# A transformer block in split fp32: planned operation list, transposed copy of x, parameters as columns

## The chip, the cores and the metric

One core of one Trainium2 chip runs the whole block. The metric is device time in microseconds (us), the median of the runs; lower is better. The core has five engines with a queue of their own each: TensorE (PE, matrix products), VectorE (DVE), ScalarE (ACT), GpSimd (POOL) and SyncE (SP), which here only issues DMA transfers. Each works its queue in order.

## The reference

The input x is 256 rows of 2048 channels. Three residual steps follow one another.

```python
f = swiglu(rmsnorm(h, ln_ffn1_pre), ffn1_gate, ffn1_up, ffn1_down)   # 2048 -> 5632 -> 2048
h = h + 0.5 * rmsnorm(f, ln_ffn1_post)
p = rmsnorm(h, ln_mix_pre) @ w_in           # RWKV-7 input, pooling input, two gates
y_a = rwkv7(p[...]) @ w_proj_a              # a scan over 256 steps, 16 heads of 64
y_b = pool(p[...]) @ w_proj_b               # moving averages over 2, 4, 8, 16 rows
m = sigmoid(g_a) * y_a + sigmoid(g_b) * y_b
h = h + rmsnorm(m @ w_out, ln_mix_post)
f = swiglu(rmsnorm(h, ln_ffn2_pre), ffn2_gate, ffn2_up, ffn2_down)
h = h + 0.5 * rmsnorm(f, ln_ffn2_post)
```

All is float32. rmsnorm(x, g) divides each row by the root of its mean square and multiplies channel by channel with g.

## The kernel before

**A product in three parts.** PE multiplies in a rounded format (F32R). Every operand is split: ACT copies it into F32R ("high", `wH`, `xH`), DVE subtracts that from the original ("low", `wL`, `xL`), and `mm3` (L178 to L180) sums high x high, high x low and low x high in one PSUM bank. So a weight tile of 128 x 1024 costs one DMA of 512 KB on SP's queue (L140), one ACT copy (L154) and one DVE subtraction (L155), for 12 matmuls of 128 x 512 on PE.

**Transposed activations.** PE wants the rows of an activation by channels. `transpose_split` (L635 to L648) turns a piece of 128 x 512 with four PE transposes, and ACT (L641) and DVE (L643) read the result out of PSUM, scaled by the gain, as high and low. Inside the feed-forward stages the hidden activations are turned on DVE instead (L653) and moved by 16 small POOL DMAs a block (L665).

**The head.** Gate block 0 of the first feed-forward is written out in `head`: 12 warm-up transposes (L514), then loads of x in pieces of 256 KB, of the gain row g1 (L1561), which one more PE transpose makes a column, and of the weights, and then for each pair of channel tiles the transposes of x between the matmuls. After its last matmul the row statistics follow (eight ACT sums of squares, L725).

**Seven products for eight.** From feed-forward block 2 on (there are 11 blocks of 512 hidden columns), `seven` computes the gate and up columns of a block together and replaces some groups of eight 128 x 512 products by seven on sums and differences of the operands (Strassen's scheme; DVE makes the differences of the weights, L407 to L415, and ACT and DVE split them, L422 and L423). At the end of such a block DVE adds the banks together (L449), the product with Silu (L750) follows, and then the turn. The banks of the gate half (`f0`, `f1`) are those that the next block starts on.

**The order of work.** In the feed-forward stages the order on PE, ACT and DVE is written out by a small planner: PE's work is a list with durations (`put`), all other operations are events with a time on PE's clock (`at`), and `run` merges the two. The times are constants written by hand (for instance, the additions at a block's end at 0.7 us after the last group of seven, `AHEAD`, `CARRY`, `TURNS`). A weight tile's load, copy and subtraction are one event, at the time when a buffer comes free (`slot`: five split buffers `WS_BUFS`, four raw ones `W32_BUFS`). `run` is called once in each stage's first product. The rest (the mixer's ACT and DVE work, the products after it) is ordered by the compiler's scheduler.

**The offloaded pair.** In blocks 3 to 6 of each feed-forward (`PROBE`), one of the ten plain weight pairs does not use DVE for its low part (`low_by`, L326 to L348): its raw tile, high and low parts lie in buffers of their own; ACT copies the high part (L335). In the first feed-forward ACT also writes the negated tile (L337) and a POOL DMA accumulates onto it (L341); in the second POOL subtracts (L343).

**Parameters.** Gains and RWKV vectors come by a dozen small DMAs as rows, and two PE transposes (L936) make columns of them (`load_rows`).

Of the kernel before, what the change touches and what calls it, by code (L numbers as in the profile page):

```python
# [11 lines left out]
F32 = mybir.dt.float32  # L12
# [6 lines left out]
P = 128  # L19
# [19 lines left out]
TT = 0.45  # L39
NUNITS = 33  # L40
STAG = 10
TRAIL = 16
AHEAD = (5.0, 6.0)
TURNS = [[4.2, 5.3, 6.4, 7.5], [5.3, 6.0, 6.7, 7.4]]
WARM = 12
TB = 4
DOWN = ((0, 7, ((8, 12), (0, 3, 5, 7, 9)), 0),
        (2, 8, ((2, 4, 6, 8, 10, 12), (0, 2)), TRAIL))
OUT = ((0, 0, (), 0), (1, 2, ((4,), (0,)), 0), (3, 0, (), TRAIL))
FAST = range(2, 11)  # L50
PROBE = range(3, 7)
CARRY = (18, 21)
NG, SPOTS = 3, ((2, 4), (1,))

ROWS = [("ln_mix_pre", 16), ("ln_ffn2_pre", 16), ("mu", 26), ("w0", 8), ("a0", 8),
        ("k_k", 8), ("k_a", 8)]
ROWS2 = [("r_k", 8), ("gn_w", 8), ("gn_b", 8), ("pool_scale", 8)]


class Block:  # L60
    def __init__(s, tc, ctx):
# [5 lines left out]
        s.late, s.after, s.items, s.events, s.now = [], [], deque(), [], 0.0  # L67
        s.clk, s.uses = 0.0, []
# [35 lines left out]
    def at(s, t, fn):  # L104

        s.n += 1
        heapq.heappush(s.events, (t, s.n, fn))

    def slot(s, end):

        s.uses.append(end)
        n = len(s.uses) - 1 - WS_BUFS
        return s.uses[n] if n >= 0 else n - 1.0

    def run(s):

        s.now = 0.0
        E = mybir.EngineType
        with s.tc.manual_schedule(engines={E.PE, E.Activation, E.DVE}):
            while s.items or s.events:  # L120
                while s.events and (s.events[0][0] <= s.now or not s.items):
                    heapq.heappop(s.events)[2]()
                if s.items:
                    t, fn = s.items.popleft()
                    fn()
                    s.now += t
            s.stats()
        s.now = s.clk = 0.0
        s.uses = []

    def put(s, t, fn):
        s.items.append((t, fn))
        s.clk += t
# [48 lines left out]
    def gemm_tok(s, w, c0, at, KT, evac, lead=False, trail=False, xs=None, hold=False,  # L182
                 order=None):
        pss = [s.pm.tile([P, 512], F32, tag="mm", name=s.nm("mm")) for _ in range(2)]
        ws = {}

        def do(k, h):
            (wH, wL), (xH, xL) = ws[k], at(k)
            s.mm3(pss[h], xH[:, h * P:h * P + P], xL[:, h * P:h * P + P], wH, wL,
                  k == 0, k == KT - 1)  # L190

        def keep(tiles):
            ws.update((k, (wH, wL)) for k, wH, wL in tiles)

        def both(k0, k1):
            for k2 in order or range(k0, k1, 4):
                keep(s.load_w(w, k2, min(4, k1 - k2), c0, 512))
                for k in range(k2, min(k2 + 4, k1)):
                    do(k, 0)
                    do(k, 1)  # L200

        if trail:
            both(0, KT - TRAIL)
            s.by_half(w, c0, KT - TRAIL, KT, s.clk, AHEAD[0], do, keep,
                      lambda h: evac(h, pss[h]))
            return
        k0 = 0
        if xs:
            s.head(w, c0, KT, do, keep, xs)
            k0 = KT  # L210
        elif lead:
            s.by_half(w, c0, 0, STAG, s.clk, AHEAD[1], do, keep)
            s.run()
            k0 = STAG
        both(k0, KT)
        if hold:
            for h in range(2):
                s.at(0.3 + 1.6 * h, lambda h=h: evac(h, pss[h]))
            return
        with s.tc.high_priority(offset=BOOST):  # L220
            for h in range(2):
                evac(h, pss[h])

    def gemm_at(s, w, c0, at, KT, evac):

        pss = []
        ws = {}

        def load(k):
            ws.update((i, (wH, wL)) for i, wH, wL in s.load_w(w, k, 2, c0, 512))  # L230

        def do(k):
            if not pss:
                pss.extend(s.pm.tile([P, 512], F32, tag="mm", name=s.nm("mm"))
                           for _ in range(2))
            for h in range(2):
                (wH, wL), (xH, xL) = ws[k], at(k)
                s.mm3(pss[h], xH[:, h * P:h * P + P], xL[:, h * P:h * P + P], wH, wL,
                      k == 0, k == KT - 1)
        for k in range(0, KT, 2):  # L240
            s.at(s.slot(s.clk + 12 * MM), lambda k=k: load(k))
            s.put(6 * MM, lambda k=k: do(k))
            s.put(6 * MM, lambda k=k: do(k + 1))
        for h in range(2):
            s.at(s.clk + 0.3 + 1.6 * h, lambda h=h: evac(h, pss[h]))

    def by_half(s, w, c0, k0, k1, start, ahead, do, keep, done=None):

        for k in range(k0, k1, 2):
            s.at(start + (k - k0) * 3 * MM - ahead,  # L250
                 lambda k=k: keep(s.load_w(w, k, 2, c0, 512, k - k0 >= STAG)))
        for h in range(2):
# [1383 lines left out]
```

## Time and profile before

| what | us |
|---|---|
| median of 3 runs (2049.80 to 2051.21) | 2050.68 |
| profiled execution, span from first to last instruction | 2047.8 |
| PE busy | 2019.4 |
| DVE busy | 1741.7 |
| ACT busy | 1161.5 |
| POOL busy | 337.8 |

The profiled execution's span is 2.9 us below the median of the timed runs, which holds what lies around the first and last instruction. The views of the trace used below are: the page (busy time of each engine), the table of stretches (busy time, instruction counts, the granted TensorE clock as a share of full speed, share of DMA engines and GB/s for each stretch of time), the list of waits (who waited for whom), and the timeline (start, duration, engine, line, operation, output<-inputs, count, and in square brackets the idle time before it with what ended it). A matmul's stated duration covers its way through the array; the next one starts earlier, so PE can lose time between two matmuls that the busy share does not show. The distance between starts shows it.

### The profile page before, as it was taken

What the parts mean: (1) busy time and instruction counts of PE and PEld (TensorE: products, weight loads), DVE (VectorE), ACT (ScalarE), POOL (GpSimd) and SP (SyncE); (2) the same over time, 40 slices, a digit from 0 to 9 for tenths busy, and PEclk for the clock granted to TensorE, in tenths of its full rate; (3) what the DMA queues carried; (4) which work ended last, traced back from release to release, by engine and by line L of the source; (5) the groups of instructions that cost most, each with busy time, mean ns of one, the idle gap of its engine ahead of it and who ended that gap; (6) DMA issues with size and microseconds to landing.
All of it is one profiled execution on the core that took longest, in us unless ns stands there. A gap on an engine that the chain in (4) does not pass through costs nothing.

```text
span 2047.8 us, 28810 instructions
## 1 busy us (share of the span) xinstructions
PE 2019.4 (99%) x10011; PEld 1664.0 (81%) x10011; DVE 1741.7 (85%) x2296; ACT 1161.5 (57%) x1563; POOL 337.8 (16%) x681
## 2 busy tenths in 40 slices
PE   9999999999999999999999999999999999999997
PEld 7887778888888888878788788888877888888886
DVE  6998889999998867789689577869989999999986
ACT  7555555555555566675576444565555555555553
POOL 0122111211000023402320111001222213110000
PEclk9999999999999999999999999999999999999999
DMA  7667776666667777757556557666666666766674
GB/s 259 194 202 240 219 219 211 203 220 212 207 213 257 226 212 213 205 162 213 147 171 187 162 170 265 216 216 195 213 200 213 215 198 213 219 215 195 216 258 144
DMA packets 227418, 425.66 MB, mean 208 GB/s; under 512 B 24127, under 2 KB 27593, under 8 KB 227273
## 3 DMA queue, kind: packets, MB, share of 16 engines
q1 hardware_dynamic: 204137, 384.70, 60.4%
q0 software_dynamic: 22848, 38.61, 6.1%
q8 instruction: 79, 1.29, 0.3%
q10 hardware_dynamic: 288, 0.52, 0.1%
q14 instruction: 66, 0.54, 0.1%
HBM read 396.69 MB, written 8.39 MB: 198 GB/s over the span
## 4 chain that ended last, share of the span: by engine, by line
PE 81%; DVE 8%; issue 4%; DMA 3%; ACT 2%; POOL 0%; DVEq 0%; ACTq 0%; POOLq 0%; SPq 0%
PE mm L178 23%; PE mm L180 23%; PE mm L179 23%; PE ms L179 3%; PE ms L180 3%; PE ms L178 3%; DVE wL L155 2%; DMA w<-in_ffn_gate_dram 2%; DVE u L449 1%; DMA w<-in_ffn_up_dram 1%; ACT wH L154 1%; DVE t L407 1%; DVE wL L423 1%; ACT wH L422 1%; PE tr L635 1%
## 5 line engine op out<-in xcount | busy, mean ns | idle before, releaser
L178 PE MATMUL mm<-wH,xH 128*128 128x512 f32 x2200 | 859.4, 391 | 4.8 <-DVE u L449 3.7
L179 PE MATMUL mm<-wL,xH 128*128 128x512 f32 x2200 | 855.3, 389 | 5.0 <-DVE wL L155 5.0
L180 PE MATMUL mm<-wH,xL 128*128 128x512 f32 x2200 | 854.6, 388 | 0.7 <-DVE xL L643 0.7
L155 DVE TENSOR_TENSOR wL<-w,wH 128x1024 fp32r<-128x1024 f32 (+1 forms) x543 | 655.2, 1220 | 205.7 <-ACT wH L154 199.6
L154 ACT CAST wH<-w 128x1024 fp32r<-128x1024 f32 (+1 forms) x543 | 557.9, 1044 | 342.5 <-PE mm L180 245.1
L178 PEld LDWEIGHTS mm<-wH,xH 128*128 128x128 f32 x2200 | 413.4, 188 | 94.4 <-issue 6.8
L179 PEld LDWEIGHTS mm<-wL,xH 128*128 128x128 f32 x2200 | 413.5, 188 | 90.6 <-DVE wL L155 8.3
L180 PEld LDWEIGHTS mm<-wH,xL 128*128 128x128 f32 x2200 | 413.4, 188 | 86.2 <-DVE xL L643 1.5
L422 ACT CAST wH<-t 128x1024 fp32r<-128x1024 f32 x172 | 181.1, 1054 | 291.9 <-DVE t L415 172.0
L665 POOL DMA_DIRECT2D x<-T x352 | 173.0, 502 | 687.7 <-DVE T L653 317.2
L423 DVE TENSOR_TENSOR wL<-t,wH 128x1024 fp32r<-128x1024 f32 x172 | 209.6, 1221 | 10.9 <-ACT wH L422 6.4
L423 DVE TENSOR_TENSOR wL<-w,wH 128x1024 fp32r<-128x1024 f32 (+1 forms) x172 | 163.1, 948 | 1.1 <-ACT wH L422 1.1
L422 ACT CAST wH<-w 128x1024 fp32r<-128x1024 f32 (+1 forms) x172 | 140.6, 832 | 30.5 <-DMA w<-in_ffn_down_dram 15.3
L407 DVE TENSOR_TENSOR t<-w,w 128x1024 f32<-128x1024 f32 x86 | 104.8, 1218 | 2.5 <-DMA w<-in_ffn_down_dram 2.5
L179 PE MATMUL ms<-wL,sH 128*128 128x512 f32 x174 | 67.7, 389 | 0.0
L178 PE MATMUL ms<-wH,sH 128*128 128x512 f32 x174 | 67.7, 389 | 0.0
L180 PE MATMUL ms<-wH,sL 128*128 128x512 f32 x174 | 67.7, 389 | 0.0
L449 DVE TENSOR_TENSOR u<-ms,u 128x512 f32<-128x512 f32 x92 | 61.4, 686 | 1.4
L718 POOL DMA_DIRECT2D R<-R x96 | 47.2, 499 | 83.8 <-issue 57.6
L411 DVE TENSOR_TENSOR t<-w,t 128x512 f32<-128x512 f32 x86 | 58.9, 685 | 0.0
L415 DVE TENSOR_TENSOR t<-w,t 128x512 f32<-128x512 f32 x86 | 58.8, 684 | 0.0
L845 POOL DMA_DIRECT2D gb<-in_ln_ffn_post_dram x4 | 2.2, 558 | 284.7 <-PE mm L180 142.6
(333 smaller groups left out, 2068.2 us busy)
## 6 DMA issues: line engine op xcount, KB each, us to landing
w<-in_w_in_dram SPq DMA_DIRECT2D x128, 512.0 KB
w<-in_ffn_up_dram SPq DMA_DIRECT2D x122, 512.0 KB
w<-in_ffn_gate_dram SPq DMA_DIRECT2D x120, 512.0 KB
w<-in_ffn_down_dram SPq DMA_DIRECT2D x116, 512.0 KB
w<-in_ffn_down_dram SPq DMA_DIRECT2D x120, 256.0 KB
w<-in_ffn_gate_dram SPq DMA_DIRECT2D x112, 256.0 KB
w<-in_ffn_up_dram SPq DMA_DIRECT2D x108, 256.0 KB
w<-in_w_out_dram SPq DMA_DIRECT2D x28, 512.0 KB
```

The costliest lines, as they stand in the source:

```text
L154: s.nc.scalar.copy(vH, v)
L155: s.nc.vector.tensor_tensor(out=vL, in0=v, in1=vH.bitcast(F32), op=ALU.subtract)
L178: nc.tensor.matmul(ps, aH, bH, start=start, stop=False)
L179: nc.tensor.matmul(ps, aH, bL, start=False, stop=False)
L180: nc.tensor.matmul(ps, aL, bH, start=False, stop=stop)
L407: V.tensor_tensor(out=v["t13"], in0=v["a"], in1=v["b0"].to_broadcast([P, 2, 512]), op=ALU.subtract)
L411: V.tensor_tensor(out=v["t24"][:, 0], in0=v["a"][:, 0], in1=v["t13"][:, 1], op=ALU.add)
L415: V.tensor_tensor(out=v["t24"][:, 1], in0=v["b"][:, 0], in1=v["t24"][:, 0], op=ALU.subtract)
L422: nc.scalar.copy(H, v[n_])
L423: V.tensor_tensor(out=L, in0=v[n_], in1=H.bitcast(F32), op=ALU.subtract)
L449: V.tensor_tensor(out=u[o], in0=bank[b], in1=u[i], op=ALU.add)
L665: nc.gpsimd.dma_start(out=x[0][q * 32:q * 32 + 32, i], in_=src[i * 32:i * 32 + 32, q])
```

## The change

The order of PE's matmuls in the products is the same, and so are the numbers of the groups of seven, the buffers and the tile sizes. Different are:

- **The planner.** Every operation is a `job` with an engine, a duration from a formula, the jobs that it needs, the buffers that it takes and gives back, and a due time. `play` runs a small simulation: each of ACT, DVE, POOL and the loads takes, when free, the ready job with the earliest due time; PE takes its list in order. The order in which jobs were taken is the order in which they are issued. Two lists make up the kernel: the first feed-forward with its border into the mixer's first gate product, and the second half of `w_proj_a` with the output projection and the second feed-forward. Load, copy and subtraction of a weight tile are jobs of their own, as are the sum of squares and the mean of the row statistics, which come due 9 us after the piece that they read. The sums of the additions that free `f0` and `f1` have due times 1.0 and 1.6 us after a block's last matmul.
- **The offloaded pair is gone**: `low_by` and `PROBE` are removed, and all ten pairs of a block go through ACT and DVE.
- **The head.** A second copy of x, laid out by channels (`x_t`), is an input. `head` loads it in pieces, ACT and DVE make high and low parts of 128 x 256 straight from it, and no PE transposes stand between the matmuls. x itself (2 MB) is loaded after the gate weights, for the row statistics only.
- **Parameters** come as one laid-out array of columns (`cols`): 16 columns in a first DMA on ACT's queue, the other columns in a second; the transposes are gone.
- **Normed activations** of the first feed-forward are made from `x_t` (four DVE operations of 128 x 256) in place of high plus low and a product (two of 128 x 1024), and the sums for the groups of seven read them directly.

The core of the diff:

```diff
+LAG = dict(P=0.2, A=0.18, V=0.16, G=0.2, D=2.4, N=0.0)
+CAPS = dict(w=W32_BUFS, ws=WS_BUFS, u=1)
+FAST = {b: "fffqffqllqlll" for b in range(2, 11)}
-FAST = range(2, 11)
-PROBE = range(3, 7)
+va = lambda m: 0.07 + m / 960
+aa = lambda m: 0.09 + m / 1200
...
+    def play(s, order, wait):
+        free = dict(P=0.0, A=0.0, V=0.0, G=0.0, D=-10.0)
...
+        while True:
+            best = None
+            for e in "DAVG":
+                if now[e]:
+                    t = free[e]
+                elif soon[e]:
+                    t = max(free[e], soon[e][0][0])
+                else:
+                    continue
+                if best is None or t < best[0]:
+                    best = t, e
+            if order and not order[0].left:
+                t = max(free["P"], order[0].ready)
+                if best is None or t < best[0]:
+                    best = t, "P"
...
+            n.left = -1
+            free[e] = t + n.dur
+            n.fn()
+            done(n, t + n.dur + n.lag)
...
+    def feed(s, w, k, n, c0, t, hold=False):
...
+        g = s.job("D", 1.75 * m / 1024, get, t - 9, take=("w", b))
+        h = s.job("A", aa(m), high, t - va(m) - aa(m) - 0.5, (g,), None if hold else ("ws", b))
+        return b, s.job("V", va(m), low, t - va(m) - 0.3, (h,), give=(("w", b),))
...
         def pair(k, w, c0, b):
-            if other and (b, k) == other[1]:
-                s.low_by(other[0], w, k, c0, s.clk, keep)
-            else:
-                s.at(s.slot(s.clk + 12 * MM), lambda: keep(s.load_w(w, k, 2, c0, 512)))
+            ws, l = s.feed(w, k, 2, c0, s.clk)
...
+        t = s.clk + 1.0
+        j1, j2, j3, j4 = m
+        a0, a1 = plus(1, "f0", 1, t, j3, last["f"]), plus(3, "f1", 3, t + 0.6, j4, last["f"])
+        s.freed.update(f0=a0, f1=a1)
...
+        def part(k):
+            H, L = [u[:, k % 4] for u in uT[k // 4]]
+            v = xT[k // 4][:, k % 4]
+            nc.scalar.activation(out=H, in_=v, func=AF.Copy, scale=g[:, k:k + 1])
+            nc.vector.scalar_tensor_tensor(out=L, in0=v, scalar=g[:, k:k + 1],
+                                           in1=H.bitcast(F32), op0=ALU.mult,
+                                           op1=ALU.subtract)
...
             ps = s.psum("warm")
             for _ in range(WARM):
-                s.nc.tensor.transpose(ps[:, :P], s.ident, s.ident)
-            load(0, 0)
-            load(1, 0)
-            load(None, None)
+                nc.tensor.transpose(ps[:, :P], s.ident, s.ident)
             get(0, 1)
+            x(1, 1)
             get(1, 1)
-            get(2, 1)
-            get(3, 1)
+            x(2, 2)
+            get(2, 2)
+            for k in range(4, KT, 4):
+                x(k, 4)
+                get(k, 2)
+                get(k + 2, 2)
+            x(None, None)
...
-        s.gemm_tok(w_in, GB, at, NKD, ev_sig(lambda h: sgb0[:, h]), lead=True)
+        s.lead(w_in, GB, at, NKD, sig, lambda k, h: uj[k // 4, h])
+        s.run(MORE[0])
...
+        nc.scalar.dma_start(out=c0, in_=cols[:, :16])
+        load(0, 1)
+        nc.scalar.dma_start(out=ct[:, 16:], in_=cols[:, 16:])
```

In these lines `MM` is 0.2265 us, the planner's time for one matmul of 128 x 512; in the order string of a block, f and l are plain pairs of the gate and up half, q is a group of seven.

More of the change, by code (lines that the diff above doesn't have):

```diff
@@ L66, in __init__ @@
         s.nxt = None
[L67 to L68 removed]
+        s.late, s.after = [], []
+        s.clk, s.order, s.asks, s.freed, s.jobs = 0.0, [], {}, {}, []
         s.cp = E(tc.tile_pool(name="cp", bufs=1))
```

1210 lines of the change are left out of this document (671 added, 539 removed).

## The prediction

> **What bounds the kernel now.** I read the page first, then the table of stretches, the list of waits, and the timeline at the places which these name.
>
> ```profile
> span 2047.8 us, 28810 instructions
> PE 2019.4 (99%) x10011; PEld 1664.0 (81%) x10011; DVE 1741.7 (85%) x2296; ACT 1161.5 (57%) x1563; POOL 337.8 (16%) x681
> ```
>
> PE is busy for 99%, so the work on PE itself sets the end; the change leaves the matmuls of the products as they are. What can be won is time in which PE loses its rhythm. Its rhythm shows where nothing disturbs it, and the stages with groups of seven show how far they fall short:
>
> ```profile
> 100.00:350.00 250.00, 246.19 (x1078) 201.29 (x1077) 226.40 (x258) 141.10 (x163) 50.89 (x100) 1.00 0.71 219
> 350.00:480.00 130.00, 129.60 (x572) 106.96 (x571) 123.64 (x142) 73.34 (x85) 23.52 (x48) 1.00 0.69 216
> 500.00:690.00 190.00, 190.00 (x840) 157.39 (x839) 171.62 (x193) 110.36 (x128) 3.28 (x6) 1.00 0.69 223
> 1420.00:1640.00 220.00, 215.62 (x938) 176.43 (x936) 200.91 (x222) 120.01 (x137) 48.87 (x84) 0.99 0.66 209
> 1640.00:1830.00 190.00, 189.39 (x836) 156.90 (x837) 179.69 (x209) 105.97 (x122) 39.23 (x80) 1.00 0.68 213
> 1577.50:1581.00 3.50, 2.84 (x8) 2.25 (x9) 3.50 (x4) 0.93 (x2) 0.00 (x0) 0.72 0.49 125
> ```
>
> After the stretch and its length come PE's busy time with its matmuls in brackets, then weight loads, DVE, ACT and POOL in the same way, the granted clock, the DMA share and GB/s. In 500 to 690 PE does 840 matmuls in 190 us, 0.2262 us each. At that rate 1078 matmuls take 243.8 us, so 100 to 350 loses 6.2 us. In the same way 350 to 480 loses 130 - 129.4 = 0.6 us, 1420 to 1640 loses 220 - 212.2 = 7.8 us, and 1640 to 1830 loses 0.9 us. That is 15.5 us in the two stages of blocks 2 to 10, nearly all of it in the first blocks of each, which are those with the offloaded pair. What ends PE's waits:
>
> ```profile
> PE mm L179 <- DVE wL L155: 5.0, 6, 1.9
> PE mm L178 <- DVE u L449: 3.7, 8, 0.9
> ```
>
> The first kind waits for the low part of a weight, the second, eight times, for the additions at a block's border. Now one of the first kind, in the second feed-forward:
>
> ```profile
> 1573.50 1.05 ACT L335 CAST dH<-w 128x1024 fp32r<-128x1024 f32 x1 [2.82 <-DMA w<-in_ffn_up_dram]
> 1574.46 1.99 ACT L154 CAST wH<-w 128x1024 fp32r<-128x1024 f32 x2
> 1574.64 2.39 POOL L343 TENSOR_TENSOR dL<-w,dH 128x1024 fp32r<-128x1024 f32 x1 [6.91 <-ACT dH L335]
> 1575.54 3.70 DVE L155 TENSOR_TENSOR wL<-w,wH 128x1024 fp32r<-128x1024 f32 x2 [3.60 <-ACT wH L154]
> 1575.84 0.39 PE L178 MATMUL mm<-wH,xH 128*128 128x512 f32 x1
> 1578.16 0.50 PE L179 MATMUL mm<-wL,xH 128*128 128x512 f32 x1 [1.94 <-DVE wL L155]
> 1579.33 0.63 PE L180 MATMUL mm<-wH,xL 128*128 128x512 f32 x1
> 1579.76 0.63 PE L178 MATMUL mm<-wH,xH 128*128 128x512 f32 x1
> ```
>
> The offloaded pair's copy (`dH`, L335) stands in ACT's queue and waits 2.82 us for its own late load; behind it stand the copies of plain weights (L154), which DVE waits for, 3.60 us; PE's next matmul begins 2.32 us after the one before it, 2.1 us late. Then the rows of matmuls are 0.43 us apart for a while (1579.33 to 1579.76), and the stretch 1577.5 to 1581 has a granted clock of 0.72. The first feed-forward has the same picture:
>
> ```profile
> 289.63 1.05 ACT L335 CAST dH<-w 128x1024 fp32r<-128x1024 f32 x1 [2.87 <-DMA w<-in_ffn_up_dram]
> 290.58 1.05 ACT L337 ACTIVATE dL<-w 128x1024 fp32r<-128x1024 f32 x1
> 292.60 2.36 DVE L155 TENSOR_TENSOR wL<-w,wH 128x1024 fp32r<-128x1024 f32 x2 [4.59 <-ACT wH L154]
> ```
>
> **The change, part by part. The offloaded pair.** A wait costs more than its bracket, since a matmul's 0.39 us cover the start of the pause: at the border below the distance of starts is 0.74 us, 0.51 lost, and the bracket says 0.35. So the eight border waits cost about 3.7 + 8 x 0.16 = 5.0 us, and 10.5 of the 15.5 us are left for late weights, for the slow clock after 1578, and for small change. With `low_by` gone, ACT's queue has no copy in it that waits for a load ahead of its time in front of copies that are due: loads are started 9 us ahead and ACT takes what is ready. I take 8 us off and leave 2.5. The price is DVE's: one more subtraction in four blocks of each feed-forward.
>
> ```profile
> 172.94 3.56 DVE L155 TENSOR_TENSOR wL<-w,wH 128x1024 fp32r<-128x1024 f32 x3
> ```
>
> Three take 3.56 us, so each costs 1.19 us of DVE. In 350 to 480, where no pair is offloaded, DVE is busy 123.64 of 130 us, 95%, and PE loses 0.6 us. A block lasts 183 x 0.2262 = 41.4 us on PE (61 products of three matmuls: 40 for the ten channel tiles that are multiplied in the plain way, with two row halves and two column halves each, and 21 for three groups of seven), so DVE has 39.4 us of work in it and 2.0 us to spare. That is the cover: on those rows the eight blocks pay nothing for the extra 1.19 us. If the cover is gone they pay at most 8 x 1.19 = 9.5 us.
>
> **The borders.** A border as it is:
>
> ```profile
> 182.79 1.28 DVE L449 TENSOR_TENSOR u<-mm,u 128x512 f32<-128x512 f32 x2
> 182.88 0.39 PE L180 MATMUL mm<-wH,xL 128*128 128x512 f32 x1
> 183.62 0.47 PE L178 MATMUL mm<-wH,xH 128*128 128x512 f32 x1 [0.35 <-DVE u L449]
> ```
>
> The addition that frees the bank of the next block's first matmul begins when the old block's last matmul does. The new due time of this addition is 1.0 us after the block's end, which is late by itself; but DVE takes it whenever nothing ready is due earlier, and the subtractions that are due earlier are limited by five split buffers, so most additions will come before the border. Between none and all of the 5.0 us I take half, 2.5 us. The free choice of DVE has a risk: the order is fixed by modelled durations, and one late load holds a whole queue. For such new stalls I put 1.0 us (bounds 0 and 5, the last as much as the borders cost now).
>
> **The head.**
>
> ```profile
> 6.94:33.49 26.55, 24.66 (x96) 17.61 (x97) 0.00 (x0) 0.00 (x0) 1.00 0.76 273
> 13.04 0.39 PE L180 MATMUL mm<-wH,xL 128*128 128x512 f32 x1
> 13.27 0.60 PE L635 MATMUL tr<-ident,x 128*128 128x128 f32 x4
> 13.62 0.48 PE L178 MATMUL mm<-wH,xH 128*128 128x512 f32 x1
> 13.94 0.40 PE L179 MATMUL mm<-wL,xH 128*128 128x512 f32 x1
> ```
>
> The first row is the table of stretches for the products' matmuls alone: the 96 of gate block 0 take 26.55 us where 96 x 0.2262 = 21.7 would do, 4.8 us too many. A turn of four transposes costs, from the start of the matmul ahead to the second one behind, 0.90 us where two matmuls would take 0.45, so 0.45 us; six such turns lie in this stretch, 2.7 us. The other 2.1 us are waits of the first two channel tiles for weights and low parts. How the beginning stands:
>
> ```profile
> 0.81 0.39 SPq L1561 DMA_DIRECT2D g1rows<-in_ln_ffn_pre_dram  x1
> 1.26 4.72 DMA w<-in_ffn_gate_dram
> 6.01 0.62 ACT L154 CAST wH<-w 128x512 fp32r<-128x512 f32 x1 [2.99 <-DMA w<-in_ffn_gate_dram]
> 6.66 0.69 DVE L155 TENSOR_TENSOR wL<-w,wH 128x512 fp32r<-128x512 f32 x1 [1.69 <-ACT wH L154]
> 6.95 0.49 PE L178 MATMUL mm<-wH,xH 128*128 128x512 f32 x1
> 1.73 2.82 PE L514 MATMUL warm<-ident 128*128 128x128 f32 x12 [1.73 <-POOL ident masks.py:199]
> 4.69 1.03 PE L635 MATMUL tr<-ident,x 128*128 128x128 f32 x4
> 2035.57 0.39 PE L180 MATMUL mm<-kH,xL 128*128 128x512 f32 x1
> ```
>
> (The row of 1.26 is from the chain of waits, the others from the timeline; the last is the tail's, for below.) The first weight becomes the first entry of SP's queue, in place of the gain row, so it comes 0.4 us earlier, and with it all that follows (its way from issue to landing, 4.72 us, stays). The turns go, 2.7 us. Of the 2.1 us I take 0.6 off: the parts made from `x_t` no longer wait for PE, but the second weight tiles of 512 KB arrive no sooner. Sum 3.7 us (bounds 1.0 and 5.2). The low bound comes from the clock: the turns from 4.69 us on keep PE at work between the warm-up, which ends at 4.55, and the first matmul; without them PE is idle for some 1.9 us there, nearly as long as the pause after 1575.84 that slow matmuls followed. [...]
>
> **What moves beside it.** The 2 MB of x for the statistics are new traffic between the gate weights and the up weights on SP's queue.
>
> ```profile
> 10.00:20.00 10.00, 10.00 (x52) 8.26 (x52) 7.89 (x19) 6.49 (x16) 0.00 (x0) 1.00 1.05 389
> 13.10 0.38 SPq L140 DMA_DIRECT2D w<-in_ffn_up_dram  x1
> ```
>
> At 389 GB/s they take 5.4 us. Up weights are issued from 13.10 us now, and are first needed at 33.5, so they have some 10 us in hand: nothing is lost; without that cover PE would wait 2 us. The Silu of block 0 now waits for the statistics, and behind it on ACT stand copies; its banks are next needed by block 1's gate, 96 matmuls or 21.7 us later, and the statistics are due by 15 us: nothing. The later statistics of the other two borders free ACT at the border and are needed a whole product later; the store of each piece (POOL) comes after the piece as before: nothing. The two parameter transposes on PE and a dozen tiny SP issues go, worth under 0.5 us, left out. Mixer and tail keep their chains; at the tail PE's last matmul starts at 2035.57 and the end is 12.2 us later by the span; I take no change, bounds 1 us either way.
>
> Sum: 8.0 + 2.5 + 3.7 - 1.0 = 13.2 us off the profiled 2047.8, so a span of 2034.6. The median of the runs lies 2.9 us above the profiled span (2050.68), and I keep that distance: 2037.5 us.
>
> **The rivals.** (a) The plan is as good as it looks on paper: all 15.5 us go, and the head gives its 5.2. That is 20.7 off, 2030.0. For it: 500 to 690 loses nothing with DVE at 90%. Against: 350 to 480 still loses a border with no offloaded pair. (b) The head gives nothing because PE runs cold: with the row of 1579.33 (0.43 us apart) for 8 to 16 matmuls, 1.6 to 3.3 us are lost there; only about 1 us of the head's gain is left, so 2040.2. For it is the missing work between 4.69 and 6.9; against, that the next weights bound that stretch anyway. [...] (c) The list does what the old one did: offloaded stalls go, but as many come back where a job runs later than modelled; only the head's 3.7 is left: 2047.0. (d) The other side: DVE becomes the bound of blocks 2 to 10. It has 39.4 us of work in a block of 41.4. From 2.0 us of idle time a block on, every further microsecond of DVE waiting on a late copy or load costs PE one, 18 times. The waits are there to be had: DVE waited for ACT's L154 4.59 us at one place above. With 3.5 us idle a block, blocks last 42.9; they now average 41.4 + 15.5 / 18 = 42.3, so 0.6 x 18 = 11 us more, less the head's 3.7: 2058.0. Against it stands the row 350 to 480. (e) The order on the lists could be the old order with new names; then only the head and the offloaded pair count, 11.7 us off: 2039.0, inside the forecast.
>
> **How the numbers follow.** Runs of this kernel differ by 0.07% (2049.80 to 2051.21), so about 0.2%, 4.1 us, is what can be told from no change: faster means below 2046.6, slower above 2054.8. Forecast with (e), 2033 to 2042: 0.48. (a) 0.16; (b) 0.13; (c) 0.14, a third of it faster; (d) 0.09. Faster: 0.48 + 0.16 + 0.13 + 0.05 = 0.82; same 0.09; slower 0.09. The range leaves out (d) and the far end of (a) and (c): 2029 to 2049.
>
> **What would show it.** No operation on `dH`; in 100 to 350 a count of about 1100 matmuls in place of 1078, and over 960 in 220 us of the second feed-forward; waits of L178 for u below 2 us in all; no stretch with a clock under 1.00 after the head; no `tr<-ident,x`, and gate block 0 over at about 29.8 us. It is wrong if DVE in the blocks is at 95% or more while PE's counts stay at 431 in 100 us (that is (d)), or if new waits of PE name other jobs of DVE or loads in the same number (c).

## The result, and the profile after

The changed kernel takes 2038.15 us (median of 4 runs, 2036.29 to 2041.18) against 2050.94 (4 runs, 2049.80 to 2051.68) for the one before: a ratio of 0.9943, 95% interval 0.9929 to 0.9957. The profiled execution has a span of 2036.3 us, 11.5 less than before (2047.8). From the page of the changed kernel:

```profile
span 2036.3 us, 28634 instructions
PE 2013.3 (99%) x9976; PEld 1661.5 (82%) x9976; DVE 1730.9 (85%) x2288; ACT 1161.7 (57%) x1542; POOL 323.8 (16%) x671
```

The busy shares tell nothing of it, as before. The table of stretches of the changed kernel, to be held against the rows of the prediction (columns as there), does. Its first row is the head:

```profile
6.94:33.49 26.55, 25.52 (x99) 20.57 (x100) 20.28 (x29) 19.38 (x32) 0.00 (x0) 1.00 1.01 379
100.00:350.00 250.00, 250.00 (x1104) 207.09 (x1103) 235.27 (x268) 143.20 (x162) 47.13 (x96) 1.00 0.69 214
350.00:480.00 130.00, 128.99 (x565) 105.41 (x564) 120.58 (x139) 72.58 (x82) 23.56 (x48) 1.00 0.68 211
1420.00:1640.00 220.00, 220.00 (x972) 182.19 (x971) 207.11 (x237) 124.27 (x142) 42.53 (x87) 1.00 0.68 211
1640.00:1830.00 190.00, 189.51 (x835) 156.31 (x835) 177.39 (x208) 107.96 (x126) 36.02 (x74) 1.00 0.69 214
```

In the head's 26.55 us there are 99 matmuls now, where the kernel before did the 96 of gate block 0 and its transposes. From 100 to 350 there are 1104 matmuls where there were 1078, and 972 from 1420 to 1640 where there were 938: both stretches now run at 0.2263 to 0.2265 us a matmul, with next to no loss. But 350 to 480 has 565 where it had 572, so something new is lost there. The list of PE's waits says where to look; the eight waits for `u` are gone from it:

```profile
PE mm L270 <- ACT wH L246: 3.4, 1, 3.4
...
PE tr L716 <- DVE sga L1295: 1.5, 1, 1.5
...
PE ms L271 <- DVE wL L504: 1.2, 2, 0.8
```

The last of these rows leads to 410 us. The timeline of the changed kernel there:

```profile
402.12 1.06 ACT L500 CAST wH<-t 128x1024 fp32r<-128x1024 f32 x1 [0.39 <-DVE t L485]
...
409.19 0.62 ACT L757 CAST xH<-x 128x512 fp32r<-128x512 f32 x1 [6.02 <-DMA x<-T]
...
409.72 1.05 ACT L500 CAST wH<-t 128x1024 fp32r<-128x1024 f32 x1
...
410.80 1.23 DVE L504 TENSOR_TENSOR wL<-t,wH 128x1024 fp32r<-128x1024 f32 x1 [0.27 <-ACT wH L500]
...
412.08 0.50 PE L271 MATMUL ms<-wL,sH 128*128 128x512 f32 x1 [0.76 <-DVE wL L504]
```

The reader has seen this picture in the prediction with another name in it: a copy on ACT (`xH`, L757, of the hidden activations that POOL's DMAs have moved) stands first in the queue and waits 6.02 us for its transfer; behind it stands the copy of a weight (L500), then DVE's subtraction, then PE. The planner took 4.0 us for the landing of these transfers (`lag` in `carry`). And the head, where the first row of the list leads:

```profile
0.81 0.44 SPq L232 DMA_DIRECT2D w<-in_ffn_up_dram  x1
...
1.30 0.47 SPq L232 DMA_DIRECT2D w<-in_ffn_gate_dram  x1
...
1.72 2.82 PE L615 MATMUL warm<-ident 128*128 128x128 f32 x12 [1.72 <-POOL ident masks.py:199]
...
5.61 1.28 ACT L607 ACT_TABLE_LOAD   x1 [5.61 <-DMA xT<-in_x_t_dram]
...
6.90 0.51 ACT L607 ACTIVATE xH<-xT,gains 128x256 fp32r<-128x256 f32 x1
...
7.32 0.60 ACT L246 CAST wH<-w 128x512 fp32r<-128x512 f32 x1
...
7.97 0.79 PE L270 MATMUL mm<-wH,xH 128*128 128x512 f32 x1 [3.43 <-ACT wH L246]
...
13.55 0.63 PE L270 MATMUL mm<-wH,xH 128*128 128x512 f32 x1
13.98 0.44 PE L271 MATMUL mm<-wL,xH 128*128 128x512 f32 x1
```

The first matmul starts at 7.97 us, a microsecond later than before (6.95), and from 9.29 to 13.98 us the matmuls are 0.43 us apart. The prediction had gate block 0 over at about 29.8 us; here the 97th matmul, the first behind it, starts at 32.87.

To place gains in one kernel against another I took all matmuls with 512 columns, of which every kernel here has the same 8,382, and compared the time at which the n-th of them starts. The table shows by how much the distance from one mark to the next is shorter (-) or longer (+) than in the kernel before, in us; "blocks" are the two stages of seven products for eight, the mixer part is the stretch from about 850 to 960 us, and the last column is the span. Where nothing stalls, kernels with the same code in a stretch agree there to a few hundredths of a microsecond. Where they stall they can differ by more, up to 1.1 us in the second blocks of the changed kernel and e1 to e3, and the old head gives between -0.30 and 0.39, the old tail between -0.63 and 0.03.

| kernel | head, to n=200 | first blocks, to 2000 | to 3600 | mixer part, to 4000 | to 5800 | second blocks, to 7400 | rest | span |
|---|---|---|---|---|---|---|---|---|
| changed | -1.02 | -4.27 | -0.09 | 0.01 | 2.21 | -7.30 | -0.99 | 2036.3 |
| e1_warm | -3.28 | -4.08 | -0.09 | 0.01 | 2.30 | -6.44 | -1.00 | 2035.2 |
| e2_table | -1.94 | -4.43 | -0.09 | -0.01 | 4.17 | -6.55 | -0.99 | 2037.9 |
| e3_warm_table | -3.30 | -4.37 | -0.11 | 0.01 | 2.25 | -6.17 | -1.00 | 2035.1 |
| e4_no_offload | -0.19 | -6.33 | 0.01 | -3.65 | -0.02 | -8.37 | -0.63 | 2028.6 |
| e5_lag | -2.40 | -6.63 | -0.13 | -0.01 | 0.39 | -8.37 | -1.00 | 2029.6 |
| e6_late_copy | -0.30 | -5.73 | 0.01 | 0.00 | -0.01 | -3.03 | -0.29 | 2038.4 |
| e7_dve_more | 0.11 | 3.45 | 0.31 | 0.02 | -0.01 | 2.17 | -0.62 | 2053.2 |
| e8_combo | -3.40 | -6.63 | -0.11 | 0.00 | 0.39 | -8.37 | -1.00 | 2028.6 |
| e9_lag9 | -3.17 | -6.64 | -0.12 | -3.65 | 0.59 | -8.37 | -0.99 | 2025.4 |
| e10_dma_both | 0.39 | -5.69 | 0.01 | -0.01 | -0.01 | -6.43 | 0.03 | 2036.1 |
| e11_stats_now | -3.33 | -6.64 | -0.36 | -0.01 | 0.87 | -8.37 | -0.66 | 2029.3 |

### The profile page after: what moved, and what is told of

It reads as the page before. It is cut to its first block, busy times and chain, and to the rows that moved or that the text cites. A ratio compares the mean times of both kernels' runs of the same rounds, so it can differ in the third digit from the quotient of the medians.

```text
span 2036.3 us, 28634 instructions
## 1 busy us (share of the span) xinstructions
PE 2013.3 (99%) x9976; PEld 1661.5 (82%) x9976; DVE 1730.9 (85%) x2288; ACT 1161.7 (57%) x1542; POOL 323.8 (16%) x671
## 3 DMA queue, kind: packets, MB, share of 16 engines
q8 instruction: 78, 1.28, 0.3%
## 4 chain that ended last, share of the span: by engine, by line
PE 92%; DVE 3%; issue 2%; DMA 1%; ACT 1%; POOL 0%; DVEq 0%; ACTq 0%; POOLq 0%
PE mm L270 26%; PE mm L271 26%; PE mm L272 26%; PE ms L271 4%; PE ms L272 4%; PE ms L270 4%; DMA sga<-T 1%; DVE wL L295 1%; DMA w<-in_ffn_gate_dram 0%; PE pA L1539 0%; DVE wL L504 0%; PE tr L716 0%; ACT wH L500 0%; DVE fg L1007 0%; DVE wL L247 0%
## 5 line engine op out<-in xcount | busy, mean ns | idle before, releaser
L270 PE MATMUL mm<-wH,xH 128*128 128x512 f32 (+1 forms) x2232 | 873.1, 391 | 4.0 <-ACT wH L246 3.4
L271 PE MATMUL mm<-wL,xH 128*128 128x512 f32 (+1 forms) x2232 | 867.5, 389 | 0.2
L272 PE MATMUL mm<-wH,xL 128*128 128x512 f32 (+1 forms) x2232 | 867.2, 389 | 0.3 <-DVE xL L725 0.3
L295 DVE TENSOR_TENSOR wL<-w,wH 128x1024 fp32r<-128x1024 f32 x391 | 470.9, 1221 | 93.5 <-ACT wH L289 87.6
L289 ACT CAST wH<-w 128x1024 fp32r<-128x1024 f32 x391 | 407.0, 1053 | 249.1 <-PE mm L272 152.9
L500 ACT CAST wH<-t 128x1024 fp32r<-128x1024 f32 x172 | 181.1, 1053 | 221.8 <-DVE t L493 112.9
L247 DVE TENSOR_TENSOR wL<-w,wH 128x1024 fp32r<-128x1024 f32 (+2 forms) x159 | 188.0, 1191 | 76.3 <-ACT wH L246 74.7
L246 ACT CAST wH<-w 128x1024 fp32r<-128x1024 f32 (+2 forms) x159 | 162.5, 1026 | 140.1 <-PE mm L272 118.8
L500 ACT CAST wH<-w 128x1024 fp32r<-128x1024 f32 (+1 forms) x172 | 143.1, 834 | 71.5 <-PE mm L272 32.4
L504 DVE TENSOR_TENSOR wL<-w,wH 128x1024 fp32r<-128x1024 f32 (+1 forms) x172 | 163.7, 952 | 4.7 <-ACT wH L500 4.6
L540 DVE TENSOR_TENSOR u<-mm,u 128x512 f32<-128x512 f32 x92 | 61.1, 683 | 11.2 <-PE mm L272 11.2
```

The lines of the kernel that those rows point to most:

```text
L246: s.nc.scalar.copy(vH, v)
L247: s.nc.vector.tensor_tensor(out=vL, in0=v, in1=vH.bitcast(F32), op=ALU.subtract)
L270: nc.tensor.matmul(ps, aH, bH, start=start, stop=False)
L271: nc.tensor.matmul(ps, aH, bL, start=False, stop=False)
L272: nc.tensor.matmul(ps, aL, bH, start=False, stop=stop)
L289: s.nc.scalar.copy(b["H"][:, :m], b["t"][:, :m])
```

## The experiments

The theory at the outset: the blocks gain because the offloaded pair is gone, they give back some at the new stalls, and the head gains little because PE runs slow there and the ACT table is loaded late. The rivals: it is the list's order that gains and not the missing pair (then the old order without the pair lacks room on DVE), and the head is bound by its loads whatever PE and ACT do.

**The head: warm-up and table.**

```diff
-WARM = 12
+WARM = 36        # e1_warm; 28 in e3_warm_table
```
```diff
 with s.tc.manual_schedule(engines={E.PE, E.Activation, E.DVE, E.SP}):
+    nc.scalar.copy(s.small(1, "tab"), s.mhalf[:, :1])   # e2_table, e3_warm_table
     ps = s.psum("warm")
```

> 36 warm-up transposes in place of 12, nothing else. Theory 1 (the new head loses its gain because PE has nothing to do between the warm-up and the first matmul at 7.97 us, and then runs its first 14 matmuls 0.43 us apart): PE is at full clock at the first matmul, the first 14 are 0.23 apart, and gate block 0 ends about 2.2 us earlier (its 97th matmul at 30.7 in place of 32.87). Rival (the loads and splits of the second to fourth tiles bound the head, not the clock): matmuls 0.23 apart, but waits for wL or wH in their place, and the 97th matmul at 32.3 or later.

Measured: 2037.09 us, one run. The timeline of this kernel's PE:

```profile
1.72 5.73 PE L615 MATMUL warm<-ident 128*128 128x128 f32 x36 [1.72 <-POOL ident masks.py:199]
7.91 0.49 PE L270 MATMUL mm<-wH,xH 128*128 128x512 f32 x1 [0.46 <-ACT wH L246]
8.63 0.50 PE L271 MATMUL mm<-wL,xH 128*128 128x512 f32 x1 [0.23 <-DVE wL L247]
8.97 0.39 PE L272 MATMUL mm<-wH,xL 128*128 128x512 f32 x1
9.20 0.40 PE L270 MATMUL mm<-wH,xH 128*128 128x512 f32 x1
```

The first matmul comes at the same time, but the next follow at 0.23 us and not at 0.43. The 97th matmul starts at 30.60 us, where the changed kernel has 32.87 and the one before 33.50: 2.27 us were the slow matmuls of that trace. The span falls only by 1.1, because the second blocks lost 0.9 more, in stalls like that at 410.

> One ACT copy of 128x1 ahead of the head, which needs no DMA, nothing else. Theory: ACT's function table (1.28 us at 5.61) loads early, as in the kernel before (at 1.74), so the first matmul comes at 6.7 in place of 7.97. The first matmuls stay 0.43 us apart, so the block's end moves by 0.3 to 1.3 us. Rival (the first weight tile lands too late, behind an up tile of 512 KB that stands first in SP's queue): the first matmul stays after 7.6.

Measured: 2039.79 us, one run. The first matmul starts at 6.81 us instead of 7.97, the 97th at 31.95, 0.92 earlier. Yet the span is 1.6 us longer than that of the changed kernel: 2.0 us were lost in front of 1240. PE's timeline of this kernel there:

```profile
1237.13 0.66 PE L717 MATMUL tr<-ident,sga 128*128 128x128 f32 x4 [1.92 <-DVE sga L1296]
...
1238.93 0.63 PE L272 MATMUL mm<-wH,yL 128*128 128x512 f32 x1
1239.35 0.63 PE L270 MATMUL mm<-wH,yH 128*128 128x512 f32 x1
```

The wait for `sga`, 1.5 us in the changed kernel, was 1.9 here, and seven distances of 0.43 us came behind it; none came behind the 1.5 us. So of the 2.0 us 0.4 were the longer wait and 1.6 the slow matmuls, and a gain of 0.9 us at the head can be lost again far behind it.

> Both: 28 warm-up transposes and the early ACT copy. If clock and table are the whole loss, gate block 0 ends 3.3 us earlier than with the change alone (97th matmul at 29.6). If the weight tiles bound what follows (the copy of the fifth and sixth tiles waited until 12.0 us for its DMA, and its low part is done at 14.3), the 97th matmul comes no earlier than 14.1 + 72 x 0.2267 = 30.4.

Measured: 2036.96 us, one run; the 97th matmul at 30.58 us, no earlier than with the warm-up alone. From ACT's timeline of this kernel:

```profile
2.24 1.28 ACT L613 ACT_TABLE_LOAD   x1 [2.24 <-issue]
...
5.62 0.51 ACT L607 ACTIVATE xH<-xT,gains 128x256 fp32r<-128x256 f32 x1 [1.90 <-DMA xT<-in_x_t_dram]
```

The table is loaded while xT is on its way, and the first copy starts 1.28 us earlier (5.62, not 6.90). Both mendings are real, but they don't add: once PE is fast, the tiles bound it (a copy of a weight waits for its load until 9.26 us, its low part is done at 11.6, and there PE waits for it, 0.76 us). So the first theory holds for 2.3 us, and the rival for what is left: no run had its 97th matmul ahead of 30.48 us.

**The offloaded pair alone.**

```diff
-PROBE = range(3, 7)
+PROBE = range(0)     # in the kernel before, nothing else
```

> The kernel before with all pairs on ACT and DVE (no offloaded pair in blocks 3 to 6), its old planner and old head. Theory (the forecast's step): the losses in 100 to 350 and 1420 to 1640, 6.2 and 7.8 us, shrink to those of the border waits, about 3 us each; 8 us off, 2043. Rival A (the planner made the gain): under 2 us off. Rival B (DVE has no room for eight more subtractions): slower, up to 9.5 us.

Measured: 2030.44 us (4 runs, 2030.29 to 2032.00) against 2053.32 for the kernel before on that chip, a ratio of 0.9892 (0.9875 to 0.9909). It was expected at 2043. One line undone in the old kernel gives more than the whole change; of the 7.7 us between the two spans 3.65 lie in the mixer part, which the line does not touch (below), and the rest still makes it worth more. The table of stretches of this kernel, and its waits for `u`:

```profile
100.00:350.00 250.00, 250.00 (x1105) 207.01 (x1104) 237.32 (x270) 142.28 (x162) 46.90 (x96) 1.00 0.69 215
350.00:480.00 130.00, 129.77 (x573) 107.03 (x572) 123.53 (x143) 73.52 (x83) 23.87 (x49) 1.00 0.69 215
1420.00:1640.00 220.00, 220.00 (x972) 182.19 (x971) 209.58 (x238) 124.59 (x142) 45.35 (x93) 1.00 0.68 213
```
```profile
PE mm L178 <- DVE u L449: 0.2, 1, 0.2
```

With the hand-written times and due times of the old order, the border waits are 0.2 us where they were 3.7. So they were no fault of the border's due time: they went with the offloaded pair, behind which DVE ran late. In the two columns of blocks 14.7 us are gained (6.33 and 8.37), and DVE does the extra subtractions without a loss: the rival that it lacks room falls.

**The new stalls.**

```diff
-ms = [s.job("G", 0.49, lambda i=i, q=q: move(i, q), t, turned, lag=4.0) for i, q in iq]
+ms = [s.job("G", 0.49, lambda i=i, q=q: move(i, q), t, turned, lag=8.0) for i, q in iq]
```

> The changed kernel with the modelled landing time of the carry's transfers raised from 4.0 to 8.0 us, so that the copies of the mixer's split (xH from x) are put later on ACT's list; nothing else differs. Theory: the changed kernel's stalls at 410.8, 454 and 1650.9 us (about 3.2 us together) arise because ACT's copy, put after a landing modelled at 4 us, stands first in its queue for 5 to 6 us with copies of weights behind it; then the waits of ACT's line 757 on a DMA fall from 5.3 to 6.0 us to under 2, those stalls go, and the span is 2033 to 2034 (2036.3 now). Rival: the moves themselves start late, because POOL waits for a free buffer, and whatever reads them is late on any list; then PE's stalls stay within 1 us of their place and the span is 2035.5 to 2037.

Measured: 2031.31 us, one run, span 2029.6. What ACT waited for ahead of the copies `xH`, in the changed kernel (us, times, longest, from its list of waits) and in this one (us, times, from the view of the tile, where no wait for `x<-T` is left and one for `sga<-T`, 2.8 us in the changed kernel, has shrunk):

```profile
ACT xH L757 <- DMA x<-T: 54.7, 19, 6.0
```
```profile
  DMA sga<-T: 1.2, 1
```

One number in the plan takes 54.7 us of waiting out of ACT's queue, and with it the 3.4 us that the blocks lost (2.36 in the first, 1.07 in the second) and 1.8 us in front of 1240. There `sga` is moved in the same way, and the changed kernel has the same picture:

```profile
1235.24 1.15 ACT L757 CAST xH<-sga 128x512 fp32r<-128x512 f32 x2 [2.77 <-DMA sga<-T]
```

Behind this copy DVE's subtraction waited 2.74 us, and behind that stood the addition (L1295) for which a transpose waited 1.5 us (the second row of the waits above). The theory holds; the rival (moves that are late on any list) falls. That is 5.3 us, more than the 3.2 of the expectation, which had left out the stall in front of 1240; the other 1.4 of the 6.7 lie in the head, whose code is the same, and are told of at the end. With the pair gone and the landing times right the blocks gain 6.63 and 8.37 us: what the old order gains by the removal (6.33 and 8.37). The new list adds at most 0.3 us to that.

**Why the pair cost so much.**

```diff
-        s.at(t - 18, high)
-        s.at(t - 17.9, low)
+        s.at(t - 11, high)      # kernel before, pair kept
+        s.at(t - 10.9, low)
```

> The kernel before, with the offloaded pair kept, but its ACT copy and its subtraction put 11 and 10.9 us ahead of the use in place of 18 and 17.9, so that the load (put 24 us ahead) has 7 us more to land. Theory: nearly all of the loss in blocks 2 to 10 comes from that copy waiting in ACT's in-order queue for its own load (2.8 us at each of the places shown, with the copies of plain weights behind it); then the copies' waits on the DMA go to nearly nothing and 9 to 14 of the some 15 us go: a span of 2034 to 2039 (2047.8 now). Rival: the pair's own work does it, POOL's subtraction slowing DVE's beside it (3.70 against 2.36 us for two) and ACT's extra copies; then the loss stays over 10 us and the span is 2043 to 2049.

Measured: 2040.11 us, one run, span 2038.4. The first blocks, where ACT and a DMA make the pair's low part, get back 5.73 of the 6.33 us that removing the pair gives; the second, where POOL subtracts, 3.03 of 8.37. In the kernel before, the copies `dH` had waited for their loads eight times (us, times, longest); in this one there is no such wait.

```profile
ACT dH L335 <- DMA w<-in_ffn_up_dram: 13.9, 8, 2.9
```

So in the first feed-forward it was nearly all the copy that waited in ACT's queue, and in the second two causes are at work. The other one, in the timeline of this kernel:

```profile
1486.57 0.68 DVE L411 TENSOR_TENSOR t<-w,t 128x512 f32<-128x512 f32 x1
...
1487.71 2.40 POOL L343 TENSOR_TENSOR dL<-w,dH 128x1024 fp32r<-128x1024 f32 x1 [11.67 <-ACT dH L335]
1487.77 2.88 DVE L415 TENSOR_TENSOR t<-w,t 128x512 f32<-128x512 f32 x1
...
1490.77 1.05 ACT L422 CAST wH<-t 128x1024 fp32r<-128x1024 f32 x1 [3.14 <-DVE t L415]
...
1491.85 0.50 PE L179 MATMUL ms<-wL,sHL 128*128 128x512 f32 x1 [0.46 <-DVE wL L423]
```

An instruction of this form took DVE 0.68 us (1486.57) and 2.88 where it started just behind POOL's subtraction: it ended at 1490.65, 0.54 us after POOL (1490.11), with 2.2 us of DVE lost; why, no run shows. It was so all four times that POOL subtracted here (three times 2.2 us, once as much with another instruction). In the kernel before it happened four times too, with 1.35 us or a little more lost each time: in the row of 1575.54 that the prediction shows, the first of the two subtractions takes 2.57 us and the second 1.21. So the later place of the copy made POOL's subtraction dearer, and this run gives the copy's part in the second feed-forward too small. The next run takes the subtraction from POOL:

```diff
-              at_tok(h2), emit, load_to(h2, lambda h: hsp[1, h]), None, "pool")
+              at_tok(h2), emit, load_to(h2, lambda h: hsp[1, h]), None, "dma")
```

> The kernel before with the offloaded pair's copy 7 us later (span 2038.4), and the pair of the second feed-forward made as in the first, by a second pass of ACT and an accumulating transfer, without POOL's subtraction. Theory: what is left of the loss in the second feed-forward (5.4 us, against 0.6 in the first) comes from POOL's subtraction, beside which a VectorE instruction of 128 x 512 took 2.88 us where 0.68 is usual, and 4.2 us of it are border waits that follow from this; then the second feed-forward loses 0.5 to 1.5 us and the span is 2033.5 to 2035. Rival: the second feed-forward is tighter for another reason (its loads or its stores); then it still loses over 4 us and the span is 2037 to 2039.

Measured: 2037.76 us, one run, span 2036.1. The second blocks get 3.4 us back (6.43 of 8.37, a loss of 1.9 where 0.5 to 1.5 was expected), so POOL's subtraction is the larger part of what was left, not all of it. The span is out of the expected range: 1 us of that is the head and the tail, which were 0.7 and 0.3 us slower with the same code (the clock records of the head show full speed from 10.87 us on and not from 4.52, see the end). What makes the last 1.9 us was not tried.

**How much room DVE has.**

```diff
-                s.at(s.slot(s.clk + 12 * MM), lambda: keep(s.load_w(w, k, 2, c0, 512)))
+                def load():
+                    keep(s.load_w(w, k, 2, c0, 512))
+                    if one_end:
+                        V.tensor_tensor(out=s.scr, in0=s.scr, in1=s.scr, op=ALU.max)
+                s.at(s.slot(s.clk + 12 * MM), load)      # on top of e4_no_offload
```

> The kernel before without its offloaded pair (span 2028.6), with one more VectorE instruction of 128 x 256 per plain weight pair in blocks 2 to 10 of both feed-forwards, ten a block, on a scratch tile; this is work that the reference doesn't have, and the outputs don't use it. At some 0.3 us each it adds 3 to 3.5 us a block. If the prediction's account of DVE holds (39.4 of 41.4 us of a block), a block then has 42.5 to 42.9 us of work and is 1.1 to 1.5 us longer, 18 times: 20 to 27 us more, a span of 2048 to 2056. If DVE has more room than that, for the reason that its waits overlap, the span stays within 5 us of 2028.6. If DVE was closer to the bound than the account has it, over 35 us more.

Measured: 2054.88 us, one run, span 2053.2, 24.6 above e4_no_offload. Of this 3.7 us lie in the mixer part (below); 9.8 lie in the first nine blocks and 10.5 in the second, 1.1 to 1.2 us a block. The table of stretches shows DVE as the bound:

```profile
100.00:350.00 250.00, 247.03 (x1079) 201.53 (x1078) 247.79 (x318) 137.00 (x158) 47.04 (x96) 1.00 0.68 209
```

DVE is busy 99% (247.79 of 250), and PE does 1079 matmuls. The timeline has the next instruction 0.33 to 0.34 us behind each extra one, so they are 3.4 us a block: 39.4 and 3.4 are 42.8 us, 1.4 more than the 41.4 of PE, and 1.1 to 1.2 came. The prediction's account of DVE, and so the price in its rival (d), holds to 0.3 us a block. It fits with this that whatever held DVE for some 2 us in a block showed at the border.

**All of it together, and the mixer.** e8_combo and e9_lag9 are the changed kernel with 28 warm-up transposes, the early copy on ACT, and the landing at 8.0 or 9.0 us.

> The changed kernel with 28 warm-up transposes in place of 12, a copy of one element on ACT ahead of everything else, and the modelled landing of the carry's transfers at 8.0 us. If the two mendings add (some 2.3 us at the head by the 97th matmul, 30.6 in place of 32.9 us, and 3.2 us of stalls after the two stage borders), the span is 2030 to 2032 and the median 2032 to 2034, still slower than the kernel before without the offloaded pair (2030.4). If the later copies only move the stalls elsewhere, the span is 2034 to 2036.

Measured: 2030.47 us (4 runs, 2030.34 to 2030.84) against 2052.87, a ratio of 0.9889 (0.9872 to 0.9907). The span is 1.4 us below the expected range. Both mendings are there in full (head -3.40, blocks -6.63 and -8.37), and the time is that of e4_no_offload, which has no new head: that one gains 3.65 us from 850 to 960 us, where neither kernel was changed. ACT's timeline of e8_combo there:

```profile
865.20 0.62 ACT L246 CAST wH<-w 128x512 fp32r<-128x512 f32 x1
867.77 0.62 ACT L246 CAST wH<-w 128x512 fp32r<-128x512 f32 x1 [1.96 <-PE mm L272]
868.30 0.36 ACT L1483 COPY R<-pV 64x256 f32<-64x256 f32 x1
```

A copy of a weight stands in the queue and waits 1.96 us for a buffer that PE still reads, and the scan's own copies (`R` from `pV`, then `zb` and `zr`) stand behind it. The order here is the compiler's, and with 9.0 us for the landing it comes out the other way:

> The changed kernel with 28 warm-up transposes, the early copy of one element on ACT, and the modelled landing of the carry's transfers at 9.0 us in place of 8.0 (which ran in a span of 2028.6). The lists of the feed-forwards hardly differ; in the mixer, where ACT and VectorE aren't on the list, the scheduler now puts ACT's copies of two 128 x 512 weights behind the copies of pV, as in the kernel before without its offloaded pair, and not ahead of them. All kernels with the other order lost 2.5 to 3.6 us at 880 to 915 us against that one. If the order of ACT in the mixer is the cause, those come back: a span of 2025.0 to 2026.2, a median of 2027 to 2028. If it is something else in the mixer, the span stays at 2028 to 2029.

Measured: 2027.15 us (4 runs, 2027.11 to 2027.34) against 2051.55, a ratio of 0.9877 (0.9861 to 0.9894), the fastest here. The same place in e9_lag9:

```profile
865.42 0.62 ACT L246 CAST wH<-w 128x512 fp32r<-128x512 f32 x1
865.94 0.51 ACT L1130 ACTIVATE zb<-R,cols 128x256 f32<-128x256 f32 x1
...
869.38 0.62 ACT L246 CAST wH<-w 128x512 fp32r<-128x512 f32 x1
869.89 0.36 ACT L1483 COPY R<-pV 64x256 f32<-64x256 f32 x1
```

The second copy comes after the gates, and the part to n = 4000 is 3.65 us shorter, to the hundredth as in e4_no_offload. The 3.65 us go with this order in both kernels that have it. All the other kernels here have the order of e8_combo. Why the compiler's scheduler turns it over stays open, and no run changed that order alone; it is luck as far as the change goes.

**The later statistics.**

```diff
-            one(h, c, ap, node, t + 9)
+            one(h, c, ap, node, t)       # on top of e8_combo
```

> The changed kernel with the two mendings of the head and the modelled landing at 8.0 us (span 2028.6), and the row statistics at the stage borders due at once in place of 9 us later. By the prediction's account (the later statistics free ACT at the border, and nothing waits for them early) they are worth nothing where ACT has room: a span of 2028.0 to 2029.5. If they stand in the way of the copies that make the next product's operand, PE waits at some of the borders (700, 1340, 1880 us) and the span is 2030 to 2034.

Measured: 2030.96 us, one run, span 2029.3, 0.6 above e8_combo: 0.5 us lost behind n = 4000 and 0.3 in the rest, 0.25 gained ahead of 3600. The later statistics are worth some half a microsecond, no more than the distance between the slowest and the fastest run of e8_combo (0.5 us).

## Why the prediction was right, point by point

The total came out close, 2038.15 for 2037.5, but most of its terms were well off and cancelled; that it came out so close is luck.

**What bounds the kernel: right.** The loss lay in the blocks with the offloaded pair and in the waits that the prediction named, and the two long stretches that hold the offloaded pair run with next to no loss now.

**The offloaded pair (-8.0) and the borders (-2.5): right in kind, too small, and not two things.** The pair alone was worth 14.7 us in the blocks (e4_no_offload), of the 15.5 that the tables had shown lost. The step that failed is the division of the 15.5 into 5.0 for borders and 10.5 for the pair, and the share taken of each (2.5 of the 5.0, 8 of the 10.5): with DVE at 39.4 of 41.4 us a block, a late start on DVE cannot be made up by the border, so the border waits were the pair's bill too. The prediction had both facts in its own text and didn't join them. Its mechanism (the copy that waits in ACT's queue) carries the first feed-forward; in the second it missed POOL's subtraction beside DVE, although its own row of 1575.54 showed DVE at 3.70 us where two subtractions take 2.36. Of the 2.1 us by which PE was late at that place, 1.35 were POOL's subtraction, and only the rest the late load.

**New stalls (+1.0): too small.** They were 3.4 us in the blocks and 1.8 in front of 1240, by the late copies of L757: 5.2 in all, just past the far bound of 5.

**The head (-3.7): wrong in size.** It gave 0.63 us by the 97th matmul and 1.02 by the 200th. Rival (b) held in its mechanism (eleven distances of 0.43 us, 2.27 us by e1_warm), and it was the prediction's own doubt; PE's pause ahead of the first matmul was 3.4 us (4.54 to 7.97) where the prediction had 1.9. The other part is the step on the first weight: it is not the first entry of SP's queue, a tile of the up weights is (0.81 us, the gate's at 1.30), and the table load, which stood at 1.74 us before, now waits behind xT:

```profile
1.74 1.28 ACT L154 ACT_TABLE_LOAD   x1 [1.74 <-PEq L1621]
```

(This row is of the kernel before.) With the warm-up mended, alone or with the table, the head gives 3.2 to 3.4 us by the 200th matmul, near to the forecast.

**What moves beside it (0): right but for the tail,** which is 1.0 us shorter, at the bound given; 0.6 of it stands in e4_no_offload too, whose tail is the old one. What the columns of parameters and the normed activations from `x_t` are worth by themselves, no run shows.

**The sum.** Blocks -11.6 (forecast -9.5 with the new stalls), head -1.0 (-3.7), the mixer with the stall in front of 1240 +2.1 (0), tail -1.0 (0): -11.5 for -13.2. The rest is the distance from span to time. In every run with both on record a time lies 1.7 to 1.9 us above the span of the same execution; the 2.9 of the prediction set a median against the span of an execution some 1 us faster, and that 1 us is not in this sum.

**The rivals.** (c) and (e) asked what the list itself does. It does the old order's work with new names: without the pair the old order loses as little in the blocks as the new one with its landing times mended. (a) came out as a bound that is reached and passed: e9_lag9 is at 2027.15, with the mixer's luck in it, and e8_combo, without it, at 2030.47. (d) did not happen, but its account of DVE was right.

## What to carry to other kernels

On an in-order queue the dear mistake is an instruction placed ahead of its input: four times here (the pair's copy, the carry's copy, the table load, the mixer's weight copy) one wait of 2 to 6 us held everything behind it, while the engine's busy share stayed at 57%. List each engine's own waits and look for the longest brackets, above all on the engine that seems to have room, and give a plan landing times with some us to spare. And undo the parts of a large change one by one: the removal of four pairs a stage was worth more than the new planner that came with it.

## What the runs showed of the hardware that was not expected

**The same head, started the same way, ran slow for different lengths.** e5_lag has the head's code of the changed kernel, and its first matmul starts at 7.87 us (7.97), yet its matmuls are fast from 11.3 us on and not from 13.98. The stretch from 8 to 14 us in the changed kernel and in e5_lag:

```profile
8.00:14.00 6.00, 6.00 (x14) 4.39 (x15) 4.97 (x8) 5.10 (x10) 0.00 (x0) 1.00 1.04 398
```
```profile
8.00:14.00 6.00, 6.00 (x19) 4.56 (x20) 4.98 (x8) 5.11 (x10) 0.00 (x0) 0.73 1.04 398
```

14 matmuls against 19: 1.3 us of the difference between these two kernels is this alone. The granted clock (third column from the end) reads 1.00 in the row with more slow matmuls and 0.73 in the other. The clock records in the traces say why: in the changed kernel the first one begins at 14.07 us, with full speed, and the column takes the time ahead of it as full too; in e5_lag the clock is full from 4.43 us, half from 7.85 to 11.26, and full again. Ahead of the first record the distance of starts is to be trusted and not that column.

The same records give the lengths. The clock stood at half speed for 3.41 us in e5_lag, for 3.41 us from 1238.61 in e2_table, and for 3.413 us from 1579.05 in the kernel before. Full speed lasted 1573.544 us ahead of the last of these and 457.386 us behind it, and 2013.864 us from 14.07 on in the changed kernel: 461, 134 and 590 times 3.4133 us. Why the matmuls were slow until 13.98 us in the changed kernel and until 11.30 in e5_lag, with 0.1 us between their starts, no run shows; as far as the change goes it is luck. Half speed followed two waits of 1.9 us (1.92 in e2_table, 1.94 in the kernel before) and did not follow the 1.5 us in the changed kernel; between these lengths nothing was tried.

**The ACT table load waited with the instruction that it belongs to.** In the changed kernel its 1.28 us stood behind the transfer (5.61 us) and not beside it; one early copy of an element moved it to 2.24 us, beside the transfer (e3_warm_table).
